# The list scheduler counts a constant beside the columns of a matmul of halves

## The chip, the cores and the metric

One core of one Trainium2 chip runs the whole program. The metric is the device time in microseconds (us) of one execution, of which three runs of the kernel before give a median. Engines are named as in the profile: PE is TensorE (matmul), PEld its weight loads, DVE is VectorE, ACT is ScalarE, POOL is GpSimd and SP is SyncE, whose queue issues nearly all DMAs.

## The reference

Two transformer-like blocks on 1024 tokens of width 1024, in float32, one layer each.

- First block: a modulated norm; a projection; chunkwise retention (4 heads, 8 chunks of 128) beside a gated delta rule (4 heads), whose state goes from chunk to chunk; an output projection; a router with a group of experts by top 1 and 2 of its 8 experts by top 2; 32 experts with gated SiLU (1024 to 512 to 1024); a residual and a norm.
- Second block: a projection; neighbourhood attention (8 heads) beside a bidirectional gated linear attention (4 heads); an output projection; an MLP 1024 to 4096 to 1024 with a squared ReLU; a final norm.

```
proj = h @ w_in[l]
...
hid = jax.nn.silu(lax.ragged_dot(xs, w1, group_sizes)) * lax.ragged_dot(xs, w3, group_sizes)
ys = lax.ragged_dot(hid.astype(xs.dtype), w2, group_sizes) * gate.reshape(-1)[order][:, None].astype(xs.dtype)
...
return jnp.square(jax.nn.relu(u)) @ w2
```

## The kernel before

**Halves.** A large float32 product is made of three matmuls: each operand x is split into hi (a copy rounded to the type fp32r, by ACT) and lo = x - hi (by DVE, sometimes by POOL), and hi·hi, hi·lo and lo·hi are added in PSUM (`mm3`, `tok_tile`, `quad_product`). These are the matmuls of halves. Nearly all have 512 columns (one PSUM bank). Smaller products (the scans, retention, routing) use plain float32 matmuls of 128 columns, and transposes through an identity.

**Stages.** They follow each other in `build`: `mixer1` (norm, projection of the delta rule, then the delta rule's chunks `dn_pre` and `dn_scan`, the token blocks `tok_blocks` and `retention`, interleaved), `mix_out` (output projection, routing, tile by tile, then `route_end`), `moe` (32 experts with weights streamed from HBM, then a loop for the rows that are left over), `mixer2` (`combine`, projections, `gla`, attention by `na_head`, output projection) and `mlp` (two halves of seven products each, after Strassen).

**The order of the work.** Nothing is emitted while the stages run. Each instruction becomes an `Op` with the engine it runs on, its predecessors (worked out from the tiles it reads and writes) and a price in ns from `price`. `flush` then plays a list schedule: of the five engines it takes the one that can start earliest on the planned clock, gives it the available op with the highest priority, moves that engine's planned clock on by the price, and makes successors available at the planned end plus a latency between the two engines. The priority is the longest priced path from the op to the end of its flush, plus a boost that the stage set (40000 for `dn_pre`, `dn_scan` and `retention`, 60000 for routing, 0 for the token blocks). So a boosted op goes in as soon as the planned clock says its input is there, and unboosted matmuls fill the time until then. The planned order of each engine becomes its instruction queue; on the chip each queue runs in order and waits on semaphores. Planned times are not kept: only the five orders are. There are two flushes: one at the end of `moe` (before its loop, which is emitted directly, without the scheduler) and one at the end of the program.

**Prices that matter here** (`price`, lines 359 to 402): a matmul of halves costs 0.4166 ns a column, at least 107 (512 columns: 213.3; 288 columns: 120.0), and 208 where it has at most 130 columns and over 64 columns of weights; twice that where fewer than 128 rows are contracted. A plain float32 matmul costs 1.68 ns a column, a transpose 107. ACT costs 55 + 0.833 a column (+40 from SBUF), a two-operand DVE op 68 + 1.042 a column, a DMA its bytes at 360 GB/s.

**Weights.** `wload` loads 128 x 2 x 512 floats (512 KB) into a ring of raw tiles and splits them into rings of hi and lo. In `moe` the loads of an expert chosen at run time are chained behind a register load.

Of the kernel before, what the change touches and what calls it, by code (L numbers as in the profile page):

```python
# [34 lines left out]
def dsize(dt):  # L35
    return 2 if dt == BF else 4
# [55 lines left out]
def elems(ap):  # L92
    n = 1
    for s, c in ap.ap[1:]:
        n *= c
    return n
# [59 lines left out]
class Program:  # L156
# [202 lines left out]
    def price(self, op, name, out, args, reads, k):  # L359
        n = elems(out)  # L360
        psum = out.tensor.name == self.pname or any(r.tensor.name == self.pname for r in reads)
        ptr = any(elems(r) == 1 for r in reads) and n > 1
        if name in ('dma_start', 'indirect_dma_start'):
            size = 1
            run = 1 << 20
            for ap in [out] + reads[:1]:
                c, last = 1, ap.ap[-1]
                if last[0] == 1:
                    c = last[1]
                run = min(run, c * dsize(ap.dtype))  # L370
                size = n * out.ap[0][1] * dsize(out.dtype)
            if name == 'dma_start':
                op.cost, op.lat = 475.0, 930.0
                op.dma = size / 360.0 * (2.0 if run < 512 else 1.0)
            else:
                op.cost, op.lat, op.dma = 1040.0, 900.0, size / 360.0
        elif op.eng == PE:
            f32 = args[0].dtype == F32
            kk, m = args[0].ap[0][1], elems(args[0])
            if name == 'transpose':  # L380
                op.cost = 107.0
            elif f32:
                op.cost = (n * 1.68 if n >= 127 else 415.0 if m > 64 else 135.0) * (2 if kk < 128 else 1)
            else:
                op.cost = max(n * 0.4166, 107.0) * (2 if kk < 128 else 1)
                if n <= 130 and m > 64:
                    op.cost = 208.0
        elif op.eng == ACT:
            op.cost = 55.0 + n * 0.833 + (40.0 if not psum else 0.0) + (93.0 if 'accum_out' in k else 0.0)
            op.table = TABLES.get(str(args[1]).split('.')[-1])  # L390
        elif op.eng == DVE:
            if name in ('tensor_scalar', 'tensor_copy', 'memset') and not psum:
                op.cost = 69.0 + n * 0.52
            else:
                op.cost = 68.0 + max(n, elems(reads[0])) * 1.042
            op.cost += 61.0 if ptr or psum and name != 'tensor_tensor' else 0.0
        elif name == 'memset':
            op.cost = 40.0 + n * 0.83
        elif 'pow' in str(k.get('op')):
            op.cost = 300.0 + n * 165.0  # L400
        else:
            op.cost = 160.0 + n * 2.0
# [2213 lines left out]
```

## Time and profile before

| | us |
|---|---|
| median of 3 runs | 2712.98 (2708.91 to 2715.82) |
| the profiled execution's own time | 2710.75 |
| span of that execution, first to last instruction | 2708.9 |
| PE busy in it | 2529.4 (93%) |
| DVE busy | 1801.0 (66%) |
| ACT busy | 1194.9 (44%) |
| POOL busy | 689.4 (25%) |
| mean granted TensorE clock | 0.980 of full |

The profile is of one execution. "Idle before" is time in which an engine's queue stood still before an instruction, with the one that released it. A busy PE is not a PE at its peak, since matmuls overlap and their ends are modelled; where PE is never idle, its pace is the count of matmuls in a stretch of time.

### The profile page before, as it was taken

The numbers are of one execution on the slowest core, as the hardware profiler recorded it, in microseconds if no ns is written. First come the engines' busy times: TensorE is split into PE (matmuls) and PEld (weight loads), VectorE is DVE, ScalarE is ACT, GpSimd is POOL, SyncE is SP. The second block draws the span as 40 slices with busy tenths as digits, with TensorE's granted clock in tenths as the row PEclk, the third lists the DMA queues.
The fourth block names the chain that finished last, engine by engine and source line by source line (L and its number), as shares of the span: only waits on it lengthen the run. The fifth ranks groups of instructions, "written<-read, shape, count | busy, mean of one in ns | idle before, by whom it ended". The sixth has DMA issues, their size and how long they took to land. (4 is left out here: it accounts for less than half of the span.)

```text
span 2708.9 us, 35429 instructions
## 1 busy us (share of the span) xinstructions
PE 2529.4 (93%) x12278; PEld 1924.6 (71%) x12278; DVE 1801.0 (66%) x2583; ACT 1194.9 (44%) x2005; POOL 689.4 (25%) x703
## 2 busy tenths in 40 slices
PE   5999999999969999999996999999999999999998
PEld 4787777886657766454444777777787888887876
DVE  8557865546679889786776344358736767578874
ACT  5234332332236677565554434247714334453332
POOL 3006541422451111322234201144213003310002
PEclk9999999999979999999998999999999999999999
DMA  7238586565349999999978442263244768787473
GB/s 254 79 118 235 175 249 189 167 205 198 133 170 340 342 347 337 351 320 364 354 263 304 138 125 92 75 195 91 69 133 162 233 221 297 282 288 239 145 249 129
DMA packets 342100, 586.30 MB, mean 216 GB/s; under 512 B 74970, under 2 KB 112526, under 8 KB 338846
## 3 DMA queue, kind: packets, MB, share of 16 engines
q1 hardware_dynamic: 335262, 567.22, 62.6%
q0 software_dynamic: 6656, 16.79, 1.8%
q8 instruction: 97, 1.59, 0.2%
q14 instruction: 85, 0.70, 0.1%
HBM read 477.40 MB, written 112.41 MB: 218 GB/s over the span
## 5 line engine op out<-in xcount | busy, mean ns | idle before, releaser
L347 PE MATMUL psum_all<-sbuf 128*128 128x512 f32 (+10 forms) x12278 | 2529.4, 366 | 167.7 <-DVE sbuf L347 102.5
L347 PEld LDWEIGHTS psum_all<-sbuf 128*128 128x128 f32 (+6 forms) x12278 | 1924.6, 176 | 772.0 <-issue 158.9
L347 ACT ACTIVATE sbuf<-sbuf 128x1024 fp32r<-128x1024 f32 (+9 forms) x894 | 816.1, 937 | 769.9 <-PE psum_all L347 355.6
L347 DVE TENSOR_TENSOR sbuf<-sbuf,sbuf 128x1024 fp32r<-128x1024 f32 (+1 forms) x592 | 725.9, 1251 | 216.0 <-ACT sbuf L347 207.5
L347 ACT ACTIVATE sbuf<-psum_all 128x512 f32<-128x512 f32 (+12 forms) x742 | 345.9, 477 | 688.8 <-PE psum_all L347 636.6
L347 POOL TENSOR_TENSOR sbuf<-sbuf 128x512 f32<-128x512 f32 (+8 forms) x353 | 446.1, 1273 | 761.2 <-DVE sbuf L347 361.4
L347 DVE TENSOR_TENSOR sbuf<-sbuf 128x1024 f32<-128x1024 f32 (+12 forms) x417 | 316.4, 778 | 108.3 <-ACT sbuf L347 31.5
L347 DVE TENSOR_TENSOR sbuf<-psum_all,sbuf 128x512 f32<-128x512 f32 (+12 forms) x290 | 171.5, 603 | 157.7 <-ACT sbuf L347 71.4
L347 DVE SCALAR_TENSOR_TENSOR sbuf<-sbuf 128x512 f32<-128x512 f32 (+5 forms) x263 | 209.3, 803 | 46.3 <-POOL sbuf L347 36.9
L347 POOL TENSOR_SCALAR sbuf<-sbuf 128x1 f32<-128x1 f32 (+3 forms) x182 | 79.7, 440 | 627.0 <-ACT sbuf L347 491.9
L347 DVE TENSOR_TENSOR sbuf<-sbuf,psum_all 128x512 f32<-128x512 f32 (+6 forms) x191 | 123.5, 663 | 118.0 <-PE psum_all L347 112.7
L347 DVE TENSOR_SCALAR sbuf<-sbuf 128x32 f32<-128x32 f32 (+7 forms) x220 | 109.5, 510 | 60.9 <-ACT sbuf L347 42.0
L1809 POOL DMA_INDIRECT y_d<-sbuf x35 | 57.4, 1641 | 195.8 <-DVE sbuf L347 194.5
L347 DVE SCALAR_TENSOR_TENSOR sbuf<-sbuf,psum_all 128x128 f32<-128x128 f32 (+1 forms) x100 | 38.2, 411 | 84.9 <-PE psum_all L347 54.1
L1797 POOL DMA_INDIRECT sbuf<-h_d,sbuf x35 | 45.1, 1288 | 186.0 <-PE psum_all L347 153.1
L347 DVE SCALAR_TENSOR_TENSOR sbuf<-psum_all,sbuf 128x128 f32<-128x128 f32 (+9 forms) x109 | 62.0, 586 | 37.9 <-PE psum_all L347 37.4
L347 POOL MEMSET sbuf<- 64x64 f32 (+10 forms) x54 | 16.9, 314 | 193.4 <-DVE sbuf L347 114.9
L347 DVE CUSTOM_DVE_ANT_0 sbuf<-psum_all,sbuf 128x512 f32<-128x512 f32 (+2 forms) x80 | 48.1, 613 | 22.3 <-PE psum_all L347 21.8
L347 POOL TENSOR_TENSOR sbuf<-sbuf,sbuf 128x1024 fp32r<-128x1024 f32 x16 | 40.9, 2561 | 40.2 <-ACT sbuf L347 39.3
L347 ACT ACTIVATE sbuf<-psum_all,sbuf 128x128 f32<-128x128 f32 (+1 forms) x72 | 24.4, 402 | 35.5 <-PE psum_all L347 23.0
L347 DVE COPY sbuf<-psum_all 128x512 f32<-128x512 f32 (+9 forms) x39 | 20.6, 528 | 22.2 <-PE psum_all L347 19.0
L347 ACT ACTIVATION_READ_ACCUMULATOR sbuf<-sbuf 128x1 f32 x152 | 28.9, 190 | 0.0
(18 smaller groups left out, 112.3 us busy)
## 6 DMA issues: line engine op xcount, KB each, us to landing
sbuf<-in_w SPq DMA_DIRECT2D x384, 512.0 KB
sbuf<-in_w_ff SPq DMA_DIRECT2D x120, 512.0 KB
sbuf<-u_d SPq DMA_DIRECT2D x64, 512.0 KB
sbuf<-in_w_in SPq DMA_DIRECT2D x56, 512.0 KB
sbuf<-in_w_ada SPq DMA_DIRECT2D x48, 512.0 KB
u_d<-sbuf SPq DMA_DIRECT2D x64, 256.0 KB
sbuf<-in_x SPq DMA_DIRECT2D x16, 512.0 KB
sbuf<-qkv_d SPq DMA_DIRECT2D x32, 256.0 KB
```

The costliest lines, as they stand in the source:

```text
L347: op = self.new_op(eng, lambda: real(*a, **k), name, reads, writes)
L1797: return self.prog.real.gpsimd.indirect_dma_start(out=xg, out_offset=None, in_=self.h2_d, in_offset=bass.IndirectOffsetOnAxis(ap=tok, axis=0),
L1809: st = self.prog.real.gpsimd.indirect_dma_start(out=self.y_d, out_offset=bass.IndirectOffsetOnAxis(ap=dest, axis=0), in_=y, in_offset=None ...
```

## The change

One line of `price`: the price of a matmul of halves becomes 0.4166 ns a column plus 13.4 ns, still at least 107.

```diff
             else:
-                op.cost = max(n * 0.4166, 107.0) * (2 if kk < 128 else 1)
+                op.cost = max(n * 0.4166 + 13.4, 107.0) * (2 if kk < 128 else 1)
                 if n <= 130 and m > 64:
                     op.cost = 208.0
```

At 512 columns the price goes from 213.3 to 226.7, at 288 from 120.0 to 133.4; up to 224 columns it stays at 107, or 208 by the line below. No instruction is added, removed or altered: the same instructions may stand in another order in each engine's queue.

## Rows read from the trace of the kernel before

**Rows 1.** The page: its line of busy times, and the granted TensorE clock in 40 equal slices of the span (tenths of full speed).

```profile
PE 2529.4 (93%) x12278; PEld 1924.6 (71%) x12278; DVE 1801.0 (66%) x2583; ACT 1194.9 (44%) x2005; POOL 689.4 (25%) x703
PEclk9999999999979999999998999999999999999999
```

**Rows 2.** Busy time by stretch, the stretches cut along the stages. Columns: the stretch, its length, busy us and count for PE, PEld, DVE, ACT, POOL, then the granted clock, the DMA share and GB/s.

```profile
180.00:580.00 400.00, 376.38 (x2217) 317.71 (x2216) 261.99 (x475) 140.12 (x420) 158.49 (x159) 0.99 0.64 197
...
600.00:620.00 20.00, 15.30 (x87) 13.47 (x88) 12.33 (x16) 9.17 (x18) 5.38 (x4) 0.89 0.76 260
620.00:640.00 20.00, 19.30 (x85) 14.39 (x85) 9.95 (x13) 5.40 (x8) 3.14 (x3) 0.86 0.62 205
640.00:760.00 120.00, 111.72 (x570) 85.31 (x568) 82.12 (x230) 27.86 (x66) 48.45 (x69) 0.99 0.41 145
760.00:820.00 60.00, 37.98 (x149) 29.24 (x148) 49.07 (x129) 24.87 (x33) 29.10 (x24) 0.69 0.53 188
820.00:1425.00 605.00, 577.66 (x2456) 349.08 (x2456) 482.24 (x558) 373.19 (x471) 134.87 (x85) 0.99 0.95 335
1425.00:1502.00 77.00, 50.41 (x217) 35.09 (x215) 50.81 (x50) 41.33 (x65) 42.26 (x57) 0.87 0.78 281
1502.00:2070.00 568.00, 557.92 (x3060) 439.68 (x3060) 276.68 (x500) 257.82 (x522) 126.51 (x186) 1.00 0.39 115
2070.00:2418.00 348.00, 347.22 (x1535) 287.30 (x1535) 243.53 (x259) 139.61 (x174) 81.99 (x52) 1.00 0.76 262
2418.00:2474.00 56.00, 50.05 (x221) 41.10 (x219) 41.28 (x39) 16.31 (x17) 0.00 (x0) 0.98 0.73 247
```

**Rows 3.** The same view in two stretches of 100 us in the MLP's first half, where all matmuls are of halves with 512 columns and 128 columns of weights.

```profile
2100.00:2200.00 100.00, 100.00 (x443) 82.81 (x442) 64.00 (x71) 29.97 (x38) 1.91 (x1) 1.00 0.64 207
...
2300.00:2400.00 100.00, 100.00 (x443) 82.67 (x442) 62.65 (x68) 47.80 (x61) 38.49 (x31) 1.00 0.83 294
```

**Rows 4.** PE in order of time in the MoE, experts of 96 rows: start, length, the group with its first form and count, and the idle time before it.

```profile
999.67 17.93 PE L347 MATMUL psum_all<-sbuf 128*96 128x512 f32 x84 [0.53 <-ACT sbuf L347]
```

**Rows 5.** Single operations of ACT and DVE in order of time, around the start of `mix_out`: splits of a weight tile (128x1024) and evacuations of one PSUM bank (128x512).

```profile
621.64 1.06 ACT L347 ACTIVATE sbuf<-sbuf 128x1024 fp32r<-128x1024 f32 x1 [1.88 <-DMA sbuf<-in_w_out]
...
622.73 1.23 DVE L347 TENSOR_TENSOR sbuf<-sbuf,sbuf 128x1024 fp32r<-128x1024 f32 x1 [0.40 <-ACT sbuf L347]
...
628.89 0.69 DVE L347 TENSOR_TENSOR sbuf<-psum_all,sbuf 128x512 f32<-128x512 f32 x1 [3.40 <-DMA sbuf<-zg_d]
...
631.66 0.60 ACT L347 ACTIVATE sbuf<-psum_all 128x512 f32<-128x512 f32 x1 [3.82 <-PE psum_all L347]
```

**Rows 6.** PE by form from 180 to 610 us (the stretch with scans, retention and token blocks).

```profile
L347 PE MATMUL psum_all<-sbuf 128*128 128x512 f32 x1025 | 264.2, 403 | 0.0
L347 PE MATMUL psum_all<-sbuf 128*128 128x128 f32 x1336 | 169.6, 278 | 24.2 <-DVE sbuf L347 9.9 <-DMA sbuf<-rq_d 5.5 <-POOL sbuf L347 4.7
```

**Rows 7.** Who PE waited for from 180 to 580 us: us in total, times, longest.

```profile
PE psum_all L347 <- DVE sbuf L347: 10.6, 13, 2.7
PE psum_all L347 <- POOL sbuf L347: 4.7, 3, 2.1
PE psum_all L347 <- DMA sbuf<-rq_d: 4.3, 3, 2.9
PE psum_all L347 <- ACT sbuf L347: 3.9, 3, 3.1
```

**Rows 8.** PE in order of time where the scans and retention end and `mix_out` begins.

```profile
600.56 10.37 PE L347 MATMUL psum_all<-sbuf 128*128 128x128 f32 x61 [1.24 <-DMA sbuf<-rq_d]
614.21 2.08 PE L347 MATMUL psum_all<-sbuf 128*128 128x36 f32 x14 [3.28 <-DVE sbuf L347]
617.16 4.10 PE L347 MATMUL psum_all<-sbuf 128*128 128x128 f32 x14 [0.86 <-DVE sbuf L347]
621.68 14.95 PE L347 MATMUL psum_all<-sbuf 128*128 128x512 f32 x64 [0.43 <-DVE sbuf L347]
636.88 11.90 PE L347 MATMUL psum_all<-sbuf 128*128 128x512 f32 x57 [0.25 <-ACT sbuf L347]
```

**Rows 9.** PE in order of time in the steady part of `mix_out`, one token tile and the start of the next.

```profile
683.61 0.44 PE L347 MATMUL psum_all<-sbuf 128*128 128x128 f32 x2 [0.24 <-POOL sbuf L347]
684.93 5.71 PE L347 MATMUL psum_all<-sbuf 128*128 128x32 f32 x36 [0.89 <-DVE sbuf L347]
690.89 10.98 PE L347 MATMUL psum_all<-sbuf 128*128 128x512 f32 x51 [0.25 <-ACT sbuf L347]
702.15 0.44 PE L347 MATMUL psum_all<-sbuf 128*128 128x128 f32 x2 [0.29 <-POOL sbuf L347]
...
709.44 10.98 PE L347 MATMUL psum_all<-sbuf 128*128 128x512 f32 x51 [0.25 <-ACT sbuf L347]
```

**Rows 10.** PE in order of time in the MLP's second half: all the waits it has there before the last matmul.

```profile
2474.06 133.22 PE L347 MATMUL psum_all<-sbuf 128*128 128x512 f32 x576 [6.01 <-ACT sbuf L347]
2610.94 7.72 PE L347 MATMUL psum_all<-sbuf 128*128 128x512 f32 x24 [3.66 <-ACT sbuf L347]
2620.57 76.47 PE L347 MATMUL psum_all<-sbuf 128*128 128x512 f32 x336 [1.92 <-ACT sbuf L347]
```

## The prediction

> **What bounds the kernel now.** I read the page first: PE is busy 93% of the span, no other engine over 66%, and the granted clock is at nine tenths or more in all but two of 40 slices [rows 1]. So PE paces most of the program, and an order of instructions can win back only PE's idle time, 2708.9 - 2529.4 = 179.5 us, and what PE does at half clock. Next I cut the span along the stages [rows 2], to see where that idle time lies and whether an order can reach it:
>
> - 180 to 580 (scans, retention, token blocks): 400 - 376.4 = 23.6 us idle.
> - 600 to 640, the end of this stage: 4.7 + 0.7 = 5.4 us idle, at a clock of 0.89 and 0.86.
> - 640 to 760 (`mix_out`): 8.3 us. 760 to 820 (the end of routing): 22 us at a clock of 0.69, where a chain of small DVE operations runs alone.
> - 820 to 1425 (MoE): 27 us, but the DMA share is 0.95 at 335 GB/s: the weights set the pace, not PE.
> - 1425 to 1502 (the sum of the experts): 26.6 us, a chain of loads, norms and transposes.
> - 1502 to 2070: 10 us in 568. 2070 to 2418 (the MLP's first half): under 1 us; nothing to win.
> - The MLP's second half: three waits of 6.0, 3.7 and 1.9 us [rows 10].
>
> The rest lies in the first 180 us and in the tail.
>
> Then I compared the prices with the trace, since the plan's order depends on nothing else. A matmul of halves with 512 columns and 128 columns of weights runs at 443 in 100 us, 225.7 ns each, with PE never idle [rows 3]: 5.8% over the old price of 213.3, and 0.4% under the new one of 226.7. In the MoE, with 96 columns of weights, 84 take 17.93 us, 213.5 ns each [rows 4]: there the old price is right and the new one 13.2 ns too high. The other engines' prices are too low as well. ACT splits a weight tile in 1.06 us for a price of 55 + 1024 x 0.833 + 40 = 948 ns (12% low) and evacuates a bank in 0.60 for 481 (25%); DVE takes 1.23 for 1135 (8%) and 0.69 for 601 (15%) [rows 5]. A DMA of 512 KB takes 524,288 B / 335 GB/s = 1.565 us where they saturate [rows 2], for a price of 1.456 (7%). So before, all engines are priced too low by 6 to 25%, and the plan's proportions are nearer to the chip's than each price. After it, PE alone is right.
>
> A rule of the Trainium skill speaks against the new price: "TensorE: Matmul & The Clock Gate", section "Back-to-back issue gap", gives the spacing of back-to-back matmuls at full clock as columns / 2.4 plus about 2.5 ns, an estimate of 215.8 ns at 512 columns, so by it the old price would be 1% off and the new one 5% too high, every filler taken away would leave a hole (term B at its upper end below), and the sum would be -6 + 13.7 + 1 = +9 us. The 225.7 above contradicts it where the weights have 128 columns; the MoE's 213.5 is near it.
>
> **The change part by part.** Nothing is executed that was not before; each term is a move in the five orders.
>
> *The filler rule.* In 180 to 610, 1025 matmuls of 512 columns and 1336 of 128 run [rows 6]. The former are nearly all token blocks without boost, and fill the time between steps of the boosted scans and retention. Those steps, counted in the code as groups of matmuls or transposes that wait for another engine: 8 x 6 in `dn_pre`, 8 x 14 in `dn_scan`, 8 x 5 in `retention`, 200 in all; so 1025 / 200 = 5.1 fillers stand ahead of each. A filler priced 13.4 ns higher fills a planned gap with fewer: 5.1 x 13.4 = 69 ns a step, 1025 x 13.4 ns = 13.7 us over the stage. Up to that much filler moves from the middle to the end.
>
> *Term A, the end of the stage gets it.* From 600 to 640 PE has little to fill with: 5.4 us idle, in waits of 1.24, 3.28, 0.86, 0.43 and 0.25 us [rows 8], and clocks of 0.89 and 0.86 mean 2 x (0.11 + 0.14) x 20 = 10 us at 1.2 in place of 2.4 GHz, right behind the waits, which cost about 5 us of PE's work. Bounds: 0 (if the filler runs out as early as now) and -10.4. I take -6, since 13.7 us of filler more than cover the waits, but some of it will be used earlier.
>
> *Term B, more waits in the middle.* PE waits 22 times from 180 to 580, 23.5 us, for DVE, POOL, ACT and the DMA of rq_d [rows 7]. Each of these grows by what is taken from ahead of it: 22 x 69 ns = 1.5 us. The other 178 steps are covered now, by at most the 1.16 us that their 5.1 fillers last; if their slack is spread evenly, 6% of them start to wait, by half of 69 ns: 0.4 us. As the links that they wait for are priced 8 to 25% low [rows 5], slack should lie nearer to zero than that; I double it and take +4. Bounds: 0, and +13.7 if every filler taken away leaves a hole.
>
> *Term C, `mix_out`.* A tile takes 709.44 - 690.89 = 18.55 us, of which PE waits 0.29 + 0.89 + 0.25 us [rows 9]. Its 48 matmuls of halves are the filler between the routing's boosted steps: 48 x 13.4 = 0.64 us, three matmuls a tile. The next tile's matmuls run in any case, so a wait grows only where a step is moved a whole matmul (0.226 us) ahead. I take one such in 4 of 7 tiles: +1. Bounds: 0 and 7 x 0.64 = +4.5.
>
> *Term D, routing's end, MoE and the experts' sum.* The chain at 760 to 820 has no halves in it. In the MoE the DMA works 95% of the time; weights are used in the order in which they are loaded, so what PE does in between is hidden behind the loads: 0. Without that cover it costs what the fourth rival prices (+9). A and B move the chosen experts' loads with them, as these start when routing ends, so they pass through in full.
>
> *Term E, second block to 2070.* PE is busy 98% there; its 10 us of waits bound a gain, and twice that is unlikely as a loss: 0, bounds -4 and +4 (half of the waits that have fillers).
>
> *Term F, MLP.* The first half is PE without a gap, its order is that of the products: 0. In the second, three waits of 11.6 us [rows 10] hang on DMA issue, as the chain of loads and subtractions from 2418 to 2474 has DMA busy at 0.73 and PE waiting at its end [rows 2]. The plan would now see PE slower and the loads with more time; it may put them earlier or other transfers between: 0, bounds -6 and +6, half of these waits either way.
>
> *Sum.* -6 + 4 + 1 = -1 us. The profiled execution would go from a span of 2708.9 to 2707.9 and from its own time of 2710.75 to 2709.8; the median of the runs lies 2.2 above that time, so 2712 is predicted.
>
> **The rivals.**
>
> - *Faster: the chain was held back by its filler.* If the scans' steps mostly have their input before PE comes to them (178 of 200 do not wait now), then taking 69 ns off each moves the scans up at no cost: B is 2, A its full -10, and the MLP's waits lose half, -6. Sum -14 to -15: 2698. For it: the measured 225.7 against 226.7, and few waits. Against: in 180 to 580 PE is already 94% busy, so moving the scans up helps only at the end.
> - *Slower: PE alone was corrected.* As all engines were priced low together, the plan now believes ACT, DVE and DMA 6% quicker against PE than before. Boosted steps go in ahead of their inputs, PE waits in order with ready fillers behind, in `mixer1` and `mix_out`. At most 13.7 + 4.5 = 18 us of holes; it makes the kernel slower beyond 0.3% once they pass 6 + 8 = 14 us while the end of the stage keeps its waits, and I price it at +14: 2727. For it: rows 5. Against: most steps have slack now.
> - *The order hardly moves.* Where PE is the bound the plan is only stretched, and the change does nothing of use: 2713. For it: 2070 to 2418.
> - *The MoE's price turns wrong.* An expert of 128 to 80 rows has 72 matmuls of halves and 12 transposes: 72 x 213.3 + 12 x 107 = 16.6 us in the old plan, below its 12 loads at 1.456 = 17.5; with 226.7 it is 17.6, so the plan takes PE for the bound, and lets ACT and DVE split weights ahead that have not landed (12 x 1.565 = 18.8 us on the chip). Evacuations then stand behind a split that waits. One split late an expert, 1.06 to 1.23 us, over some 8 such experts: +9, 2722. Against: a ring of many raw tiles and the DMA share of 0.95. [...]
>
> **How the numbers follow.** About 0.3% (8 us) is what a measurement of this kernel tells from no change. My forecast, 2712, has 0.33, with its own range of 2705 to 2720; the order hardly moving 0.06; the faster rival 0.32; PE alone corrected 0.21; the MoE 0.08. So same 0.39, faster 0.32, slower 0.29. The range reaches past the faster rival by E and a little of F, to 2692, and past the slower one to 2730.
>
> **What would show it.** Term A: less idle time and a clock near 1 in the stretch where the scans end, and token blocks' matmuls there. B: more, short waits of PE on DVE and ACT among the scans. C: a tile of `mix_out` at 18.6 to 18.8 us. D: MoE as long as before from its first chosen load to its last. F: the three waits in the MLP within 6 us of 11.6 in sum. It is wrong if a stage that I set to 0 moves by more than 6 us, above all the MoE or the MLP's second half, or if the stage to 640 us comes out more than 8 us longer or shorter.

## The result, and the profile after

The changed kernel takes 2732.90 us (median of 4 runs, 2728.39 to 2736.53) against 2711.18 for the kernel before (4 runs on the same chip): a ratio of 1.0083, 95% interval 1.0069 to 1.0097. It is slower by 0.8%, where "no change" at 2712 was forecast; the time lies above the range's upper end of 2730.

The page, its line of busy times and the granted clock, to be read against [rows 1]:

```profile
span 2731.4 us, 35479 instructions
...
PE 2535.7 (93%) x12278; PEld 1933.5 (71%) x12278; DVE 1799.9 (66%) x2583; ACT 1197.5 (44%) x2005; POOL 683.5 (25%) x703
...
PEclk9999999999989999999998999999999999999999
```

The engines' counts are the same, as they must be. The span grew by 22.5 us. PE's idle time went from 179.5 to 2731.4 - 2535.7 = 195.7 us (+16.2), and the same matmuls kept PE busy for 6.3 us more, at a lower mean clock (0.975 in place of 0.980). Where it happened is read from marks that both traces have: the store that ends a stage's last block, or its successor's first load. I take five.

| mark (us) | before | after | later by |
|---|---|---|---|
| last store of the token blocks (`zg_d`) | 614.8 | 630.5 | 15.7 |
| first steady tile of `mix_out` begins on PE | 636.88 | 652.55 | 15.7 |
| last store of `mix_out` (`h_d`) | 776.5 | 797.9 | 21.4 |
| first load of the experts' sum (`y_d`) | 1437.6 | 1458.0 | 20.4 |
| end of the span | 2708.9 | 2731.4 | 22.5 |

So 15.7 us arise before `mix_out`, 5.7 in it, and MoE, second block and MLP add 1.1 together. The windows of the changed kernel show how (columns as in [rows 2]; the last three are tiles of `mix_out`):

```profile
180.00:580.00 400.00, 366.28 (x2153) 308.30 (x2153) 252.48 (x468) 139.89 (x418) 152.94 (x157) 0.97 0.62 192
580.00:652.55 72.55, 64.48 (x335) 54.43 (x333) 32.65 (x48) 21.38 (x48) 14.16 (x13) 0.91 0.68 230
...
688.00:708.30 20.30, 18.54 (x91) 14.37 (x89) 12.27 (x35) 4.22 (x11) 7.78 (x11) 0.92 0.36 130
708.30:728.60 20.30, 18.53 (x90) 14.30 (x89) 12.30 (x35) 4.20 (x11) 7.87 (x11) 0.92 0.35 130
...
841.40:1445.40 604.00, 577.55 (x2456) 352.28 (x2456) 485.19 (x555) 374.82 (x471) 141.76 (x85) 0.99 0.95 335
```

From 180 to 580 PE is idle 33.7 us in place of 23.6, at a clock of 0.97 in place of 0.99. From 580 to the first steady tile it is idle 8.1 us, where the kernel before had 6.1 in its own stretch to 636.88. So the middle lost 10.1 us and the end gained nothing back. With 3.6 us of longer busy time (366.28 + 64.48 against 376.38 + 50.80) these make the 15.7. The MoE's line repeats that of [rows 2]: 2456 matmuls, a DMA share of 0.95, 335 GB/s.

Who PE waited for from 180 to 580, to be read against [rows 7]:

```profile
PE psum_all L347 <- DVE sbuf L347: 13.7, 7, 4.8
PE psum_all L347 <- POOL sbuf L347: 8.3, 6, 2.8
PE psum_all L347 <- ACT sbuf L347: 6.4, 3, 3.9
PE psum_all L347 <- DMA sbuf<-qkv_d: 4.4, 1, 4.4
PE psum_all L347 <- DMA sbuf<-rq_d: 0.8, 1, 0.8
```

These are 18 waits in place of 22, but the longest are 4.8, 4.4 and 3.9 us where they were 3.1 and 2.9. A boosted step now stands at the head of PE's queue for several microseconds, and PE can't reach the fillers behind it.

PE by form from 180 to 610 us shows what was taken out (against [rows 6]):

```profile
L347 PE MATMUL psum_all<-sbuf 128*128 128x512 f32 x961 | 254.3, 408 | 3.0 <-ACT sbuf L347 2.3 <-DVE sbuf L347 0.7
L347 PE MATMUL psum_all<-sbuf 128*128 128x128 f32 x1319 | 170.3, 281 | 33.7 <-DVE sbuf L347 12.9 <-POOL sbuf L347 8.3 <-DMA sbuf<-qkv_d 4.4
```

Of the matmuls with 512 columns 961 ran in it, before 1025. So 64 x 225.7 ns = 14.4 us of filler were left for later, against only 17 of the small matmuls. A count up to a fixed time falls with any idle time, so the count in PE's queue, further down, is the better witness. Where that filler went is seen in PE's order at the end of the stage (against [rows 8]):

```profile
604.42 23.09 PE L347 MATMUL psum_all<-sbuf 128*128 128x128 f32 x110 [2.99 <-DMA sbuf<-rq_d]
629.25 3.36 PE L347 MATMUL psum_all<-sbuf 128*128 128x36 f32 x16 [1.74 <-DVE sbuf L347]
635.70 16.60 PE L347 MATMUL psum_all<-sbuf 128*128 128x128 f32 x76 [3.09 <-DVE sbuf L347]
652.55 11.19 PE L347 MATMUL psum_all<-sbuf 128*128 128x512 f32 x54 [0.25 <-ACT sbuf L347]
```

The matmul of 36 columns is the key to this view. It belongs to the set-up of `mix_out` (the router's weights have 36 columns; 16 such run from 580 to 640 in the kernel before, none from 180 to 580). It stands behind the last filler, at 614.21 before and at 629.25 now, and the waits at it and behind it (before 3.28 + 0.86 + 0.43 + 0.25 = 4.8 us, now 1.74 + 3.09 + 0.25 = 5.1) belong to the set-up of `mix_out`, not to the scans. The filler pushed them 15 us down; it could not fill them.

In the steady part of `mix_out` PE's queue reads like this (against [rows 9]):

```profile
720.94 7.72 PE L347 MATMUL psum_all<-sbuf 128*128 128x32 f32 x39 [1.52 <-DVE sbuf L347]
728.91 10.79 PE L347 MATMUL psum_all<-sbuf 128*128 128x512 f32 x50 [0.25 <-ACT sbuf L347]
```

Before, two of a tile's transposes went ahead after a wait of 0.29 us, and routing's matmul of 32 columns followed after 0.89. Now the matmul of 32 columns comes first, waits 1.52 us for DVE, and the transposes stand behind it. A tile takes 728.91 - 708.63 = 20.28 us in place of 18.55, and the three tiles from 688 to 748.9 us each show a clock of 0.92. Cut into stretches of 2 us around that wait:

```profile
718.60:720.60 2.00, 0.82 (x4) 0.36 (x2) 1.89 (x7) 0.20 (x1) 1.44 (x2) 1.00 0.32 131
720.60:722.60 2.00, 1.66 (x10) 1.56 (x11) 1.82 (x14) 0.28 (x1) 0.67 (x3) 0.78 0.01 4
722.60:724.60 2.00, 2.00 (x8) 1.59 (x6) 0.07 (x1) 0.31 (x1) 0.00 (x0) 0.50 0.00 0
724.60:726.60 2.00, 2.00 (x12) 1.55 (x12) 0.00 (x0) 0.00 (x0) 0.00 (x0) 0.86 0.00 0
726.60:728.60 2.00, 2.00 (x14) 1.56 (x12) 0.69 (x1) 0.34 (x1) 0.00 (x0) 1.00 0.00 0
```

Behind the wait the clock falls to 1.2 GHz for 2 x 2 us x (0.22 + 0.50 + 0.14) = 3.4 us, though PE is busy again. At half speed that is 1.7 us of work, nearly the whole of what a tile lost. It is not so behind each such wait: the first, of 1.53 us, has no fall behind it, and its 39 matmuls take 6.16 us in place of 7.72.

```profile
681.96 6.16 PE L347 MATMUL psum_all<-sbuf 128*128 128x32 f32 x39 [1.53 <-DVE sbuf L347]
```

Of the five waits of 1.5 us and more in these tiles, it is there behind the last four (at 700.67, 720.94, 741.23 and 762.12).

The MLP's second half (against [rows 10]) has two waits of 12.1 us in sum where three had 11.6:

```profile
2496.04 132.87 PE L347 MATMUL psum_all<-sbuf 128*128 128x512 f32 x576 [5.61 <-ACT sbuf L347]
2635.38 84.06 PE L347 MATMUL psum_all<-sbuf 128*128 128x512 f32 x360 [6.47 <-ACT sbuf L347]
```

### The profile page after: what moved, and what is told of

Read it like the earlier page. It is cut to its first block, busy times and chain, and to the rows that moved or that the text cites. A ratio compares the mean times of both kernels' runs of the same rounds, so it can differ in the third digit from the quotient of the medians.

```text
span 2731.4 us, 35479 instructions
## 1 busy us (share of the span) xinstructions
PE 2535.7 (93%) x12278; PEld 1933.5 (71%) x12278; DVE 1799.9 (66%) x2583; ACT 1197.5 (44%) x2005; POOL 683.5 (25%) x703
## 5 line engine op out<-in xcount | busy, mean ns | idle before, releaser
L347 PE MATMUL psum_all<-sbuf 128*128 128x512 f32 (+11 forms) x12278 | 2535.7, 368 | 183.8 <-DVE sbuf L347 110.9
L347 PEld LDWEIGHTS psum_all<-sbuf 128*128 128x128 f32 (+7 forms) x12278 | 1933.5, 176 | 785.5 <-issue 153.2
L347 ACT ACTIVATE sbuf<-sbuf 128x1024 fp32r<-128x1024 f32 (+8 forms) x894 | 816.2, 937 | 815.8 <-PE psum_all L347 342.2
L347 DVE TENSOR_TENSOR sbuf<-sbuf,sbuf 128x1024 fp32r<-128x1024 f32 (+1 forms) x592 | 723.9, 1246 | 208.2 <-ACT sbuf L347 194.5
L347 POOL TENSOR_TENSOR sbuf<-sbuf 128x512 f32<-128x512 f32 (+8 forms) x353 | 427.9, 1222 | 795.4 <-DVE sbuf L347 373.4
L347 DVE TENSOR_TENSOR sbuf<-psum_all,sbuf 128x512 f32<-128x512 f32 (+13 forms) x290 | 171.1, 603 | 155.6 <-ACT sbuf L347 77.8
L1809 POOL DMA_INDIRECT y_d<-sbuf x35 | 64.8, 1851 | 169.7 <-DVE sbuf L347 168.3
L1797 POOL DMA_INDIRECT sbuf<-h_d,sbuf x35 | 53.0, 1514 | 180.0 <-PE psum_all L347 167.4
L347 DVE SCALAR_TENSOR_TENSOR sbuf<-psum_all,sbuf 128x128 f32<-128x128 f32 (+8 forms) x109 | 62.1, 586 | 25.0 <-PE psum_all L347 24.2
L347 DVE COPY sbuf<-psum_all 128x512 f32<-128x512 f32 (+9 forms) x39 | 20.7, 530 | 16.6 <-PE psum_all L347 13.4
```

Of the source, the lines that this page charges most:

```text
L347: op = self.new_op(eng, lambda: real(*a, **k), name, reads, writes)
L1797: return self.prog.real.gpsimd.indirect_dma_start(out=xg, out_offset=None, in_=self.h2_d, in_offset=bass.IndirectOffsetOnAxis(ap=tok, axis=0),
L1809: st = self.prog.real.gpsimd.indirect_dma_start(out=self.y_d, out_offset=bass.IndirectOffsetOnAxis(ap=dest, axis=0), in_=y, in_offset=None ...
```

## The experiments

All start from the kernel before and set the constant by stage; `half` is 0 in the stages that are not named (mix is `mixer1`, x1 is `mix_out`, out is `mlp`):

```diff
-                op.cost = max(n * 0.4166, 107.0) * (2 if kk < 128 else 1)
+                op.cost = max(n * 0.4166 + self.half, 107.0) * (2 if kk < 128 else 1)
...
+                self.prog.half = {'mix': 13.4}.get(name, 0.0); f()
```

The expectations speak of the theories as they stood: first of all that PE alone was corrected, so that fillers are now too dear against the links that they cover, in the stages where the trace shows the loss; against it, that the loss comes from another stage, or that any change of prices shuffles the order for better or worse.

**One stage at a time.** The constant in `mixer1` alone (the edit above):

> The constant of 13.4 ns is counted only in mixer1; all other stages keep the old price. Theory 1 (filler taken from ahead of steps that were priced too low leaves holes): the scans' stretch ends about 13 us later than before, as in the changed kernel (its last store to zg_d went from 614.8 to 630.5 us), a tile of mix_out takes 18.5 us again, and the whole is 9 to 15 us slower than before. Theory 2 (any reshuffle of the order costs or gains at random, in any stage): no such share; the stage's loss need not come back when the other stages keep their order. Theory 3 (the loss is all in mix_out's clock): 0 to 4 us.

2726.83 us, ratio 1.0054 [1.0036, 1.0072]: some 15 of the 22 us. Idle from 180 to 580 is 34.5 us, the first steady tile starts at 656.40, and the tiles of `mix_out` are as before, 18.5 us at full clock.

In `mix_out` alone, `{'x1': 13.4}`:

> The constant is counted only in mix_out. Theory 1 and 3 (the routing's matmul put ahead of the transposes makes one wait of 1.5 us in place of 0.3 and 0.9, and the clock drops once a tile): a steady tile takes 20.3 us in place of 18.55, the granted clock over a tile is 0.92 in place of 1.00, and the whole is 6 to 10 us slower than before. Theory 2: the tile's order may differ from that of the changed kernel, and its time with it.

2710.56 us, 1.0000 [0.9988, 1.0013], a miss. The queue has the new order, with the same waits of 1.5 us and more, but behind three of five of them the 39 matmuls take 6.15 us and behind two 7.7. The timeline shows one tile of 20.28 us and one of 18.73:

```profile
683.50 7.72 PE L347 MATMUL psum_all<-sbuf 128*128 128x32 f32 x39 [1.52 <-DVE sbuf L347]
691.47 10.80 PE L347 MATMUL psum_all<-sbuf 128*128 128x512 f32 x50 [0.25 <-ACT sbuf L347]
703.78 6.15 PE L347 MATMUL psum_all<-sbuf 128*128 128x32 f32 x39 [1.52 <-DVE sbuf L347]
710.19 10.79 PE L347 MATMUL psum_all<-sbuf 128*128 128x512 f32 x50 [0.25 <-ACT sbuf L347]
```

Behind the first wait 39 matmuls take 7.72 us, behind the second, just as long, 6.15. The windows say why, two behind each wait:

```profile
683.50:685.50 2.00, 2.00 (x11) 1.80 (x12) 1.56 (x12) 0.60 (x1) 0.43 (x3) 0.70 0.00 0
685.50:687.50 2.00, 2.00 (x9) 1.55 (x8) 0.00 (x0) 0.00 (x0) 0.00 (x0) 0.50 0.03 8
...
703.50:705.50 2.00, 1.72 (x12) 1.59 (x13) 1.81 (x14) 0.52 (x1) 0.61 (x3) 1.00 0.01 4
705.50:707.50 2.00, 2.00 (x15) 1.61 (x14) 0.00 (x0) 0.08 (x1) 0.00 (x0) 1.00 0.00 0
```

So the swapped order costs 0.2 us a tile, and a further 1.6 where the clock falls behind the wait, which it does behind one wait and not behind an equal one 20 us later.

The MoE alone, `{'moe': 13.4}`:

> The constant is counted only in the MoE, where matmuls with 96 columns of weights run at the old price (213.5 ns) and the DMA is busy at 0.95. Theory 1: nothing, within 4 us of before, since the loads set the pace. Rival (splits are planned ahead of loads that have not landed): 6 to 12 us slower, between 820 and 1430 us.

2709.04 us, 0.9992 [0.9982, 1.0002]. The fourth rival is out. (The 213.5 ns of the expectation is a mean that has transposes in it; see term D below.)

`mixer2` and `mlp` alone, `{'mixer2': 13.4, 'out': 13.4}`:

> The constant is counted only in the second block (mixer2 and mlp), which is a flush of its own. From the sum of the experts on, the changed kernel was 20 us behind at 1438 us and 22 us at the end. Theory 1: 0 to 3 us slower than before. Theory 2: anything up to 8 us either way.

2716.19 us, 1.0021 [1.0011, 1.0031]. It left no trace that can be compared, so the same kernel got a second look:

> A second look at the constant in the second block alone, which was 1.0021 of before, to see where its 5.7 us lie: in the attention and projections up to 2070 us or in the MLP's second half, whose three waits of 11.6 us in sum may differ by 6 us.

From the first load of `y_d` to the end it takes 2716.0 - 1439.4 = 1276.6 us, before 2708.9 - 1437.6 = 1271.3: +5.3. The last store of `gla_d` comes 1801.6 - 1439.4 = 362.2 us behind that load in place of 357.1, so nearly all of it lies in the projections and `gla`. In the changed kernel the same distance is 360.3 us, and that to the end is 2.1 longer than before. In this block all four engines of the two kernels have the same order of forms, so the 3.2 us between them do not come from the order in it.

All stages but `mixer1`, `{'x1': 13.4, 'moe': 13.4, 'mixer2': 13.4, 'out': 13.4}`:

> The constant of 13.4 ns in every stage but mixer1. If the stages add up: mix_out 0, MoE -2, second block +5.7, so 2 to 6 us slower than before and some 16 us faster than the changed kernel. If mix_out's tiles lock to a drop of the clock as in the changed kernel: 8 us more, and tiles of 20.3 us. Theory 1 wants the loss to be mixer1's and the tiles'.

2712.18 us, 1.0013 [1.0001, 1.0026]. Without `mixer1`'s share most of the loss is gone, though the tiles have the new order and two of them the clock's fall. The parts (0.0054 and 0.0013) add up to 0.0067, less than the 0.0083 of the whole, but the intervals allow for the difference. From 642 us on this kernel and the changed one have the same order, and still the clock falls behind two of five waits here and four of five there.

**How much constant.** Half of it, `{'mix': 6.7}`:

> Half the constant, 6.7 ns, in mixer1 alone (with 13.4 it cost 14.6 us, 1.0054). Theory 1 (every bit of filler taken from ahead of the boosted steps leaves a hole, as their own prices are too low): between, 4 to 10 us slower than before, and PE idle from 180 us to the first steady tile of mix_out between 29.7 (before) and 45.2 (with 13.4) us. Theory 2 (the order is reshuffled, and each order has its own few long waits): no relation to 13.4; anything from 6 us faster to 20 us slower.

2724.98 us, 1.0058 [1.0040, 1.0077], as much as the whole. Idle from 180 to 580 is 33.8 us. The loss isn't in proportion to the constant.

The whole and the half taken off, `{'mix': -13.4}` and `{'mix': -6.7}`:

> A constant of -13.4 ns in mixer1 alone, so that 512 columns cost 199.9 in the plan. Theory 1: more filler ahead of each boosted step, so fewer and shorter waits among the scans, PE idle from 180 us to the first steady tile below 29.7 us, and the filler runs out earlier: 4 us slower to 6 us faster than before, in no case the 14.6 us of +13.4. Theory 2: as likely as not 5 to 20 us slower, since this is as large a reshuffle as +13.4.

> A constant of -6.7 ns in mixer1 alone, between before and the -13.4 that took PE's idle time from 180 to 580 us from 23.6 to 13.1 us, and that from there to the first steady tile of mix_out from 6.1 to 17.9. Theory 1 (a price of filler sets how much idle time lies in the middle and how much at the end): 13 to 24 us idle in the middle, 6 to 18 at the end, and a time within 6 us of before. Theory 2 (reshuffles): the middle need not lie between.

2712.10 us, 1.0005 [0.9991, 1.0020], and 2720.07, 1.0031 [1.0019, 1.0042]. With cheaper fillers PE's order at the end of the stage is another one. With -13.4:

```profile
595.80 1.97 PE L347 MATMUL psum_all<-sbuf 128*128 128x36 f32 x16 [2.94 <-DVE sbuf L347]
602.82 1.11 PE L347 MATMUL psum_all<-sbuf 128*128 128x128 f32 x4 [5.05 <-DMA sbuf<-rq_d]
...
620.55 16.87 PE L347 MATMUL psum_all<-sbuf 128*128 128x128 f32 x76 [7.42 <-DVE sbuf L347]
```

The fillers are used up by 596, and retention ends with nothing beside it, in waits of 5.05 and 7.42 us. With -6.7 there is one of 10.27 us. All kernels of `mixer1` side by side, by the price of a matmul of 512 columns:

| price, ns | 512-column matmuls, 180 to 610 | idle 180 to 580 | product of 36 columns at | last store of `zg_d` (filler) | last store of `mix_d` (retention) | first steady tile |
|---|---|---|---|---|---|---|
| 199.9 | 1032 | 13.1 | 595.80 | 597.5 | 619.4 | 637.67 |
| 206.6 | 1029 | 25.7 | 613.64 | 614.9 | 639.4 | 649.00 |
| 213.3 (before) | 1025 | 23.6 | 614.21 | 614.8 | 614.1 | 636.88 |
| 220.0 | 980 | 33.8 | 627.36 | 628.6 | 622.4 | 652.61 |
| 226.7 (alone) | 962 | 34.5 | 631.12 | 632.3 | 620.4 | 656.40 |
| 226.7 (the change) | 961 | 33.7 | 629.25 | 630.5 | 618.1 | 652.55 |

Dearer filler leaves more of it undone (second column) and more idle time in the middle; cheaper filler runs out before the scans and retention (`mix_d`) are done. Before, both ended within 1 us of each other. The rows at 206.6 and 199.9 show that the price isn't a smooth knob.

PE's queue itself shows where the filler went. Count the plain matmuls and transposes of 128 x 128 from the start of the program; the table has how many 512-column matmuls stand ahead of the nth of them, and when it starts:

| nth | before | +6.7 in `mixer1` | the change |
|---|---|---|---|
| 200 | 778, 267.9 us | 768, 264.6 us | 758, 267.5 us |
| 400 | 1035, 361.2 | 995, 359.0 | 992, 360.7 |
| 600 | 1246, 447.6 | 1199, 446.9 | 1193, 445.7 |
| 1000 | 1362, 522.1 | 1325, 525.7 | 1313, 524.2 |
| 1400 | 1524, 607.7 | 1503, 617.8 | 1474, 613.0 |

By the 600th of them 53 fillers, 12.0 us, are gone from ahead of it, and it starts only 1.9 us sooner: the rest went into idle time and a lower clock. After it no more filler is taken (50 at the 1400th). Half of the constant has taken 47 by the 600th, nearly as much.

**The proportion put back.** The constant in `mixer1`, and there ACT 115 ns and DVE 92 ns an instruction dearer too, as [rows 5] has them (1060 - 948 = 112 and 600 - 481 = 119; 1230 - 1135 = 95 and 690 - 601 = 89):

```diff
-            op.cost = 55.0 + n * 0.833 + ...
+            op.cost = (170.0 if self.half else 55.0) + n * 0.833 + ...
...
+            op.cost += 92.0 if self.half else 0.0; op.cost += 61.0 if ptr ...
```

> In mixer1 alone the constant of 13.4 ns, and with it 115 ns more for each ACT and 92 ns more for each DVE operation, which is what the trace shows over their prices (1.06 for 0.948 and 0.60 for 0.481; 1.23 for 1.135 and 0.69 for 0.601 us). Theory 1: as PE's price no longer stands alone, the steps go in later, PE waits less, and the loss of 14.6 us goes, to within 5 us of before or faster. Theory 2: anything from -5 to +20 us.

2714.34 us, 1.0019 [1.0007, 1.0032]: two thirds of `mixer1`'s loss are gone. The window and the waits from 180 to 580:

```profile
180.00:580.00 400.00, 375.80 (x2196) 316.88 (x2195) 249.71 (x468) 141.72 (x420) 154.18 (x159) 0.99 0.63 193
```

```profile
PE psum_all L347 <- DVE sbuf L347: 11.0, 10, 2.2
PE psum_all L347 <- POOL sbuf L347: 6.0, 3, 3.0
PE psum_all L347 <- DMA sbuf<-rq_d: 4.0, 2, 3.0
PE psum_all L347 <- ACT sbuf L347: 2.9, 4, 1.2
```

The idle time is 24.2 us, the clock 0.99, the longest wait 3.0 us, and 1038 matmuls of 512 columns run from 180 to 610: as in the kernel before, with the dear filler. The order is not that of before: the 600th plain matmul has 1281 fillers ahead of it and starts at 459.5 us, so the steps go in later. What remains is 4.5 us at the end of the stage (first steady tile at 641.39).

The same in all stages, `half` 13.4 in each:

> In all stages the constant of 13.4 ns and with it 115 ns more for each ACT and 92 ns more for each DVE operation. Theory 1: as in mixer1 alone (1.0019), most of the loss of 1.0083 goes: 0.998 to 1.004 of before, tiles of mix_out without a wait over 1 us. If PE's price alone were not the reason: 1.005 or more.

2714.08 us, 1.0013 [0.9998, 1.0027], where the constant without it has 1.0083. In `mix_out` the waits go too: from 629 to 760 us PE has none longer than 0.35 us.

**The order within a tile.** The changed kernel with the transposes of x put ahead of routing's matmul again, by their boost; only PE's queue differs:

```diff
                 for g in (0, 4):
-                    p = self.ps([128, 4, 128], 'tq')
+                    self.prog.boost = 80000.0; p = self.ps([128, 4, 128], 'tq')
...
-                r = self.sumsq(pw, x, 'n2')
+                self.prog.boost = 60000.0; r = self.sumsq(pw, x, 'n2')
```

> The changed kernel with one edit: the transposes of x in mix_out get a boost of 80000, so that they stand ahead of the routing's matmul again; the queues of ACT, DVE, POOL and SP are the same as in the changed kernel. If that swap made the long wait and the drop of the clock in each tile: a tile of 18.5 to 18.8 us in place of 20.3, a granted clock of 0.98 to 1.00 over a tile in place of 0.92, and 6 to 9 us faster than the changed kernel, 1.005 of before. If the swap does not matter and the clock has another cause: still 20.3 us a tile and 1.008.

2725.14 us, 1.0054 [1.0030, 1.0077], the ratio of `mixer1` alone, though the intervals of this and the change overlap. The traces are sharper. The orders of ACT, DVE and POOL are the same as in the change, and PE's differs only between 682 and 767 us. A tile and the start of the next:

```profile
700.95 6.86 PE L347 MATMUL psum_all<-sbuf 128*128 128x128 f32 x39 [0.74 <-POOL sbuf L347]
708.06 10.79 PE L347 MATMUL psum_all<-sbuf 128*128 128x512 f32 x50 [0.25 <-ACT sbuf L347]
719.58 6.86 PE L347 MATMUL psum_all<-sbuf 128*128 128x128 f32 x39 [0.72 <-POOL sbuf L347]
726.69 10.79 PE L347 MATMUL psum_all<-sbuf 128*128 128x512 f32 x50 [0.25 <-ACT sbuf L347]
```

The wait is halved to 0.7 us, a tile takes 18.63 us at a clock of 1.00. From the first steady tile to the last store of `h_d` it takes 793.7 - 653.69 = 140.0 us, before 139.6, in the change 145.3. That is the 5.7 us of `mix_out`. Up to 682 us this is a second execution of the changed order: it is idle for 28.0 us from 180 to 580, in place of 33.7, yet its first steady tile begins 1.1 us later. So the idle time of one execution is not the whole loss; the rest is in the clock.

No kernel of these beats the one before beyond what can be told from it; the nearest is the MoE alone.

## Why the prediction was wrong

**What happened is the second rival**, "PE alone was corrected", given 0.21 and priced at +14 us: the plan believes the other engines quicker against PE, boosted steps go in ahead of their inputs, and PE waits in order, in `mixer1` and `mix_out`. Its price was too low: 2732.90 - 2711.18 = 21.7 us. For it speak the run in which ACT and DVE were corrected with PE (idle back from 34.5 to 24.2 us with the same filler price) and that in all stages (1.0013 in place of 1.0083), though up to 580 us these two have nearly the same order of PE, so that for `mixer1` they are one test. The fillers that are missing ahead of steps that start hardly sooner speak for it too. That any reshuffle costs time at random fits less well: with 13.4, 6.7, -6.7, -13.4 and the proportion put back, 828 to 959 places of PE's queue hold another form than before, and the ratios go from 1.0005 to 1.0058; idle time in the middle grew by 10 us with dearer filler alone, and by at most 2.1 in the three others. ACT and DVE were not corrected without PE, nor one without the other. The forecast had seen the condition in [rows 5] and answered it with a factor of two on one term.

In the terms of the sum the trace has +2.0 (A) + 10.1 (B) + 3.6 (longer busy time in the stretches of both) + 5.7 (C) + 1.1 (the rest) = 22.5 us, where the forecast had -6 + 4 + 1.

**The filler rule** was right in kind and near in size: 13.7 us of filler, 61 matmuls, were to leave the middle; in PE's queue 50 fewer stand ahead of the 1400th plain matmul (21 with half of the constant, where the rule gives 30).

**Term A (-6) is the step that failed.** It took the waits of [rows 8] for the scans' end and let the filler cover them. The 36 columns in the row at 614.21 tell that it is the start of `mix_out`, which stands behind the last filler in every kernel of the table. Idle time from 580 to the first steady tile went from 6.1 to 8.1 us, at a clock of 0.91 as before: +2 in place of -6, and the stage ended with its filler, 15.7 us later. Only the wait of 1.24 us for rq_d was retention's, and it grew to 2.99.

**Term B (+4) was mis-sized.** It measured +10.1 us of idle time (+4.4 in the second execution of the order, which lost as much in all), in sight of its upper bound of 13.7, and a clock of 0.97 in place of 0.99, which the term did not price. The step "each of the 22 waits grows by 69 ns" failed: there are fewer waits, and the longest take 3.9 to 4.8 us. Taking filler off didn't thin it evenly: 43 of the 50 were gone by the 400th plain matmul, none after the 600th, and a step that goes in too early holds up all that is behind it. Spreading the loss evenly over 200 steps can't give that. The upper end was also what the Trainium skill's spacing ("TensorE: Matmul & The Clock Gate", "Back-to-back issue gap", which gives it for a matmul by itself) would have led to, but not for its reason: with 128 columns of weights the changed kernel still runs 443 matmuls of 512 columns in 100 us (2120 to 2220), 225.7 ns each.

**Term C (+1) was mis-sized**, and its upper bound of 4.5 was too low: 5.7 us. "A wait grows only where a step is moved a whole matmul ahead" was right in kind: one step passed the transposes, and that costs about 0.2 us a tile. The tile of 20.3 us, in place of 18.6 to 18.8, comes from the clock's fall behind the wait, which the step did not price. It is there behind four of five waits, and in the runs with `mix_out` alone and with all but `mixer1`, in the same order, behind two of five, so how much of the 5.7 us another execution would show is open.

**Term D (0) was right**: 1458.0 - 797.9 = 660.1 us from the last store of `h_d` to the first load of `y_d`, before 661.1. But the reading of [rows 4] was wrong. Its 84 matmuls are 72 of halves and 12 transposes, which take less: the 72 start from 999.67 us on and the first transpose at 1016.44, so a matmul of halves takes 16.77 us / 72 = 232.9 ns with 96 columns of weights, more than the 225.7 with 128. By form, over several experts, it is 63.0 us for 264, or 239 ns, waits left out:

```profile
L347 PE MATMUL psum_all<-sbuf 128*96 128x512 f32 x264 | 63.0, 395 | 3.9 <-ACT sbuf L347 3.9
L347 PE MATMUL psum_all<-sbuf 96*128 96x96 f32 x41 | 4.2, 245 | 0.0
```

So the old price was not right there either, the new one is nearer, and the 215.8 ns that the prediction set beside this row is not near it. The sum did not hang on it.

**E (0, bounds -4 and +4)**: from the first load of `y_d` to the last store of `x_d`, which ends the second block's mixing, it takes 2089.8 - 1458.0 = 631.8 us, before 2066.2 - 1437.6 = 628.6, so +3.2, and alone 2072.3 - 1439.4 = 632.9, so +4.3: mis-sized, and at the upper bound. The same order took 632.5 and 632.4 us in the runs with all but `mixer1` and with the transposes ahead, the old order 628.0 to 630.5 in eight traces. What makes it longer was not looked for. **F (0)** was right: waits of 12.1 us for 11.6.

**The rivals.** "The chain was held back by its filler" is refuted: the last store of `mix_d` comes at 618.1, before at 614.1, so the scans did not move up. Likewise "the order hardly moves". The mark given for a wrong forecast, a stage to 640 us that is more than 8 us longer, is what the trace shows.

**What stays open.** Why half of the constant takes nearly as much filler from ahead of the first 600 plain matmuls as the whole, and why -13.4 cost nothing and -6.7 cost 8 us: which steps change places was not tried one by one. The proportion explains the direction and most of the size; that each order has its own luck of some microseconds is seen in the table as well. In a tile of `mix_out`, what decides whether the clock falls behind a wait of 1.5 us was not settled.

## What to carry to other kernels

The price list of a list scheduler is a set of proportions: in this kernel, correcting one engine to the measured duration, while the others stayed 8 to 25% low, made the plan worse where that engine's work is the filler. Correct the others from the same trace too; here that only won the loss back. A mean over a group of the timeline is not a duration until the forms in it are told apart. And before a wait is counted as fillable, read from its form which stage it belongs to: filler that is moved to the end of a stage only pushes what stands behind it.

## What the hardware showed that was not expected

A wait of 1.52 us on PE was followed by 3.4 us at 1.2 GHz, and so were four of five such waits in the changed kernel, while with the constant in `mix_out` alone one was and an equal one 20 us later was not (7.72 against 6.15 us for the same 39 matmuls). In the three tiles where the wait was halved to 0.7 us there was no fall. So a short wait can cost its own length once more in clock. What decides it is open, and a wait under 1 us is not safe from it: in the kernel before, one tile with waits of 0.90 and 0.88 us shows a clock of 0.50 from 742 to 745 us and 7.27 us for 36 matmuls that take 5.71 elsewhere.

```profile
739.86 0.44 PE L347 MATMUL psum_all<-sbuf 128*128 128x128 f32 x2 [0.90 <-POOL sbuf L347]
741.18 7.27 PE L347 MATMUL psum_all<-sbuf 128*128 128x32 f32 x36 [0.88 <-DVE sbuf L347]
```
